# LayerNorm's scale and offset behind the spatial mixing, x added by accumulating loads, and a last product in column halves

## The chip, the cores and the metric

The kernel runs on one core of one Trainium2 chip. The metric is the time of one execution in device microseconds (us), and the kernel's time is the median of several runs. Beside it there is a profile of one execution, in which the engines are called PE (matrix products), DVE (vector engine), ACT (scalar engine with activation functions), POOL (GpSimd) and SP (the engine that issues most DMAs). All of them run their own queue of instructions in order, and wait for each other by semaphores.

## The reference

One layer of a decoder trunk works on 1024 prompt rows and 8 sample rows of width 1024, all in float32. Cut to what matters here:

```
xn = rmsnorm(x, pre_g)
u, v, z_a, x_b, z_b, g_a, g_b = split(xn @ w_in)          # 7 x 1024 columns
vn = layernorm(gelu(v), ln_g, ln_b)                       # scale and offset per channel
s  = tril(w_s[h]) @ vn + b_s[h]                           # within chunks of 128 tokens, 8 channel groups h
y_a = gelu(u) * s * silu(z_a)
y_b = (blockdiag(pool(x_b)) * pool_scale) * silu(z_b)
m  = sigmoid(g_a) * (y_a @ w_pa) + sigmoid(g_b) * (y_b @ w_pb)
h  = x + rmsnorm(m @ w_out, post_g)
y  = h + rmsnorm(sigmoid(rmsnorm(h, ple_in_g) @ w_pg) * (p @ w_ple), ple_out_g)
```

Outputs are y for prompt and samples, the rows vn of the last prompt chunk and of the samples, and two pooling buffers.

## The kernel before

**Products.** Every float32 operand of a large product is cut into two parts of the reduced type float32r, a head (`split`: copied by ACT) and a remainder (subtracted by DVE), and three products of the parts are summed in PSUM. Large products use Strassen's scheme in its form with seven products (`strassen`, line 573): a pair of 128-row blocks takes seven steps P1 to P7, each a run of 24 matmuls of 258 columns (the form `Features`, channels in the partitions) or 12 matmuls of 512 columns (`Tokens`, tokens in the partitions). The sums that Strassen needs are made by DVE, on the weights before a step (`prepare`, line 478) and on the results behind it (`evacuate`, line 581). The seven products go to four regions of PSUM (`r1` to `r4`), for which there are three buffers; P2 is accumulated into the region of P1, P4 into that of P7, P3 into that of P5, so P3 can begin only when P5's result has been read.

**Stages.** The steps stand in one list: V (all four pairs), then the gate GA, U with ZA, XB with ZB, GB, the products with `w_pa` and `w_pb`, the output product (`outsteps`), and the gate product of the embedding (`gatesteps`). Other work is hung behind a step by `at(step, f)`. Weights are fetched six steps ahead (`FETCH`) and prepared three ahead (`AHEAD`).

**The mixing.** V's results are turned to token rows in `big`. In the GA stage (`flow` numbers its 28 steps and U's and ZA's first 14 from 0) every third step takes one token tile: `ln_stats` (mean and variance), `ln_apply` (line 836, two DVE passes over 1024 columns with the rows `lng` and `lnb`), then `v_split`, and `spatial` (line 885), 16 matmuls into four banks `mix` whose two halves are added by DVE, first with `bsb`, the rows of b_s. There are two banks of PSUM for such work. The samples' LayerNorm and mixing stand at `flow` 28 to 30. In the ZA stage, `done` (line 956) multiplies z by u and by the mixed rows in `big`, and `store` spills `ya`.

**The output stage.** `Out` (line 1272) handles the results of the output product: the first quarter (`direct`) is squared and summed by ACT and multiplied by the gain `post` on DVE, the three others (`summed`) are added to `u`, squared and then multiplied by the gain. `out_finish` (line 1297) loads x into `xres`, takes the reciprocal root from POOL (`rstd`), and makes h = result x rstd + x in one DVE pass. `gate_norm` squares h on ACT, takes another `rstd` and scales it to `hn`; `gate_input` transposes `hn` on PE (`pht`) and copies it to `big`. For each pair these stand behind steps 0, 1 and 6 of the next pass. In the embedding's gate product, `gated` (line 1347) takes the sigmoid, multiplies by e and sums squares by halves of 512 columns; `gate_finish` ends a tile: for tiles 0 to 5 one pass and an accumulating load of h issued by POOL, for the last two tiles passes by halves. In the last pair P2 is the last of the seven products (`LAST`).

**The order.** The program's calls aren't issued directly: `Planner` (line 53) records them with their dependencies, simulates them with a duration for each and sets the order of every engine's queue. An operation that isn't part of the fixed opening (`begin`) may start at most `LEAD` (for loads into a fresh buffer: `LOAD`) us ahead of when it is due; `rank` (line 220) picks, among those that could start at the same time, the one that is due first, where due times count for at most `PATIENCE` us behind their place in the program; `SPARE` keeps buffers back from loads. `space` (line 76) says which ranges of a tensor an operation touches. SBUF holds 46 buffers (`slot`) of 1032 columns that all stages share.

Of the kernel before, what the change touches and what calls it, by code (L numbers as in the profile page):

```python
# [21 lines left out]
QT = HT // 2  # L22
HALF = 512
EPS = 1e-6
POOL_BUF = 15
# [27 lines left out]
class Planner:  # L53
# [7 lines left out]
    TABLES = {AF.Gelu_apprx_tanh: 1, AF.Sigmoid: 2, AF.Silu: 3}  # L61
    LOAD, LEAD, PATIENCE, RATE, SPARE = 20.0, 14.0, 30.0, 0.36, 3

# [12 lines left out]
    def space(self, ap):  # L76

        dims, start = list(ap.ap), ap.offset
        if "DRAM" in str(ap.space):
            return ap.tensor.name, 0, 1, ((start, start + sum(s * (n - 1) for s, n in dims) + 1),)  # L80
# [108 lines left out]
    def order(self):  # L189
# [35 lines left out]
        while done < len(self.ops):  # L225
            best = None
            for e in self.ENGINES:
                these = ready[e]
                if fixed[e]:
                    these = [o for o in these if o is fixed[e][-1]]  # L230
                could = [(t, o) for t, o in ((soonest(o), o) for o in these) if t is not None]
                if could:
                    now = min(t for t, _ in could)
                    if best is None or now < best[0]:
                        best = now, min((o for t, o in could if t <= now + 1e-9), key=lambda o: (rank(o), o.seq))
            if best is None:
# [45 lines left out]
def hybrid_step(  # L282
# [222 lines left out]
    class Tokens:  # L505
# [4 lines left out]
        sums = (P, 2, HALF)  # L510

    class Turned(Weights):

# [59 lines left out]
    def strassen(weights, operand, user, form=Features, order=None):  # L573
# [31 lines left out]
        for p, a, b, r in sorted(plan, key=lambda x: order.index(x[0])) if order else plan:  # L605
            def run(p=p, a=a, b=b, r=r):
                new = r not in at
                if new:
                    at[r] = form.new()
                product(form, at[r], weights.ready[a], lambda k: operand.at(b, k), new, True, not new)  # L610

            steps.append(Step(lambda a=a: weights.prepare(a), run, lambda p=p: evacuate(p)))
        steps[0].loads = lambda: (weights.fetch(), user.loads())
# [221 lines left out]

    def ln_apply(t, n=P):
        v = vtok(t)
        nm, r = lnv.pop(t)
        nc.vector.scalar_tensor_tensor(out=v[:n], in0=v[:n], scalar=nm[:n], in1=lnt["g"][:n],
                                       op0=ALU.add, op1=ALU.mult)  # L840
        nc.vector.scalar_tensor_tensor(out=v[:n], in0=v[:n], scalar=r[:n], in1=lnt["b"][:n],
                                       op0=ALU.mult, op1=ALU.add)
        if t == NB - 1:
            dma(o_chunk_v[0, 0], v)
        if t == S:
            dma(o_schunk_v[0, :, 0], v[:n])

    lnt = {}

    def early_loads():  # L850
# [13 lines left out]
    def spatial_weights():  # L864

        ws = lnt["ws"]
        nc.gpsimd.affine_select(out=ws, in_=ws, pattern=[[0, NB], [-1, P]], compare_op=ALU.is_ge,
                                fill=0.0, base=0, channel_multiplier=1)
        lnt["wst"] = []
        for h4 in range(0, NB, 4):  # L870
            w = slot("wst", (P, 4, 2, P), F32R)
            ps = bank("psw")
            for i in range(4):
                nc.tensor.transpose(ps[:, i * P : (i + 1) * P], ws[:, h4 + i, :], ident)
            split(ps.rearrange("p (h t) -> p h t", t=P), w[:, :, 0], w[:, :, 1])
            lnt["wst"].append(w)

    def v_split(t):
# [6 lines left out]
    def spatial(t):  # L885

        vh, vl = lnv.pop(("cut", t))
        for h2 in range(0, NB, 2):
            ps = bank("mix").rearrange("p (h c t) -> p h c t", h=2, c=2)
            for i in range(2):  # L890
# [4 lines left out]
                nc.tensor.matmul(ps[:, i, 0], vl[:, c], w[:, 0], start=False, stop=True)  # L895
            c = slice(h2 * P, (h2 + 2) * P)
            o = big[:, t, c].rearrange("p (h t) -> p h t", h=2)
            add(o, ps[:, :, 0], lnt["bs"][:, c].rearrange("p (h t) -> p h t", h=2))
            add(o, ps[:, :, 1], o)
# [53 lines left out]
    class ZA(User):  # L953
        func = AF.Silu

        def done(self):
            u = us.pop(self.pair)
            for m, z in enumerate(self.out):
                b = 2 * self.pair + m
                mul(z, z, u[m])  # L960
                zt = z[:, :SEQ].rearrange("p (t c) -> p t c", c=P)
                mul(zt, zt, big[:, :, b * P : (b + 1) * P])
                mul(z[:, SEQ:], z[:, SEQ:], smix_s[:, b, :])
# [308 lines left out]
    class Out(User):  # L1272
# [9 lines left out]
        def direct(self, m, j, ps):  # L1282
            t = self.tile(m)
            parts[t].append(square_sum(ps))
            mul(h_of[t][:, half(j)], ps, gains["post"][:, half(j)])

        def summed(self, m, j, ps, u, free):
# [3 lines left out]
            parts[t].append(square_sum(o))  # L1291
            mul(o, o, gains["post"][:, half(j)])

# [40 lines left out]
    def out_sample():  # L1334
        start(S, "hs")
        for j, o in enumerate(sample_product(samples["m"], woop)):
            parts[S].append(square_sum(o[:NS], NS))
            mul(h_of[S][:NS, half(j)], o[:NS], gains["post"][:NS, half(j)])

# [6 lines left out]

    def gated(t, j, src):
        r = rows(t)
        g = ge[t][:r, half(j)]
        nc.scalar.activation(out=g, in_=src, func=AF.Sigmoid)  # L1350
        mul(g, e_of[t][:r, half(j)], g)
        parts[t].append(square_sum(g, r))
        if t >= NB - 2:
            mul(g, g, gains["out"][:r, half(j)])

# [18 lines left out]
    class Embed(User):  # L1374
# [3 lines left out]

        def direct(self, m, j, ps):
            gated(2 * self.pair + m, j, ps)  # L1380

        def summed(self, m, j, ps, u, free):
            t = 2 * self.pair + m
            o = ge[t][:, half(j)]
            add(o, ps, u)
            gated(t, j, o)
            if len(parts[t]) == 2:
# [7 lines left out]
    def embed_gate_sample():  # L1395
        ge_start(S)
        for j, o in enumerate(sample_product(samples["h"], wgop)):
            gated(S, j, o[:NS])
        gate_finish(S)
# [212 lines left out]
```

## Time and profile before

| | us |
|---|---|
| median of three runs | 1040.45 (1040.35 to 1040.99) |
| the profiled execution, whole | 1037.16 |
| its span, from the first to the last instruction | 1035.1 |
| PE busy, DVE busy, ACT busy, POOL busy in the span | 1007.9, 818.8, 475.3, 82.8 |
| mean clock granted to PE, as a share of full speed | 0.992 |
| mean busy share of the 16 DMA engines by the main queue | 45.4% |

The span is what the profile shows of one execution; its own time holds 2.06 us more, outside the first and the last instruction. In the rows of the profile an instruction is written as line, engine, operation, then "output<-inputs" by the names of the tiles; all recorded operations have line 275, that of `play`, so the tile's name tells them apart. A group's row ends with the busy time, the mean in ns, and the idle time of the engine just before, with what ended it. A window's row has its length, the busy time and the number of instructions of each engine, the mean clock of PE, the share of DMA and GB/s. A row in order of time has start, duration, engine, and the number of merged instructions.

### The profile page before, as it was taken

To read this page: it belongs to the slowest core of one execution; us is meant where nothing else is said; L and a number is where in the kernel's file an instruction comes from. 1 tells how busy PE (TensorE), PEld (TensorE's weight loads), DVE (VectorE), ACT (ScalarE), POOL (GpSimd) and SP (SyncE) were. 2 spreads that over 40 slices of the span, in tenths; PEclk is the share of its full clock that TensorE was granted. 3 is DMA by queue.
4 is the path that set the end of the run, shared out by engine and by line. 5 is a ranking of instruction groups with operands and counts; after the bars stand their busy time and mean duration, and the time that the engine had idled before them with its cause. 6 is when DMAs were issued, how large, how long until landed. Compare 5 with 4: busy or idle time off the path is not lost. (4 is left out here: it accounts for less than half of the span.)

```text
span 1035.1 us, 18740 instructions
## 1 busy us (share of the span) xinstructions
PE 1007.9 (97%) x7539; PEld 965.0 (93%) x7539; DVE 818.8 (79%) x1274; ACT 475.3 (46%) x844; POOL 82.8 (8%) x118
## 2 busy tenths in 40 slices
PE   8999997999999999999999999999999999998996
PEld 6999997999999999999999999999999997886885
DVE  5986557999577777776777787697699899989696
ACT  7664354444333434242323343462352364687563
POOL 2200001101000000000010100000000003312122
PEclk9999998999999999999999999999999999999998
DMA  9332564223144625612132167775695562385436
GB/s 341 123 108 86 180 205 143 83 82 109 58 155 171 225 103 164 231 46 92 62 99 100 58 229 250 282 257 204 196 338 205 193 236 83 124 296 212 123 84 203
DMA packets 85059, 169.23 MB, mean 163 GB/s; under 512 B 6370, under 2 KB 46338, under 8 KB 84965
## 3 DMA queue, kind: packets, MB, share of 16 engines
q1 hardware_dynamic: 83789, 164.36, 45.4%
q0 software_dynamic: 864, 3.15, 1.7%
q8 instruction: 59, 0.97, 0.4%
q10 hardware_dynamic: 320, 0.54, 0.2%
q14 instruction: 27, 0.22, 0.1%
HBM read 116.71 MB, written 51.77 MB: 163 GB/s over the span
## 5 line engine op out<-in xcount | busy, mean ns | idle before, releaser
L275 DVE TENSOR_TENSOR u<-acc,u 128x516 f32<-128x516 f32 x106 | 73.4, 692 | 52.1 <-PE acc L275 51.5
L275 POOL TENSOR_TENSOR rstd<-ms,mhalf 128x1 f32<-128x1 f32 (+2 forms) x45 | 56.2, 1253 | 328.2 <-DVE ms L275 325.5
L275 ACT ACTIVATE u<-acc 128x516 f32<-128x516 f32 x39 | 23.4, 600 | 70.6 <-PE acc L275 65.6
L275 ACT ACTIVATE zbw<-zbs 128x512 fp32r<-128x512 f32 x16 | 9.7, 628 | 36.4 <-DVE zbs L275 30.6
L275 POOL COPY big<-xb 128x1 f32<-128x1 f32 x8 | 3.0, 369 | 290.8 <-ACT xb L275 237.4
L275 ACT ACTIVATE paw<-pas 128x512 fp32r<-128x512 f32 x16 | 9.9, 629 | 33.2 <-DVE pas L275 27.0
L275 ACT ACTIVATE pbw<-pbs 128x512 fp32r<-128x512 f32 x16 | 10.0, 631 | 30.1 <-DVE pbs L275 23.4
L275 DVE TENSOR_TENSOR big<-big 128x1032 f32<-128x1032 f32 (+3 forms) x20 | 23.6, 1219 | 0.0
L275 PE MATMUL accm<-qh,wpoolw 128*128 128x258 f32 x128 | 21.8, 285 | 0.4 <-DVE zb L275 0.4
L275 POOL MEMSET mst<- 128x1024 f32 x1 | 1.0, 957 | 257.3 <-PE acct L275 257.3
L275 ACT ACTIVATE gaw<-gas 128x512 fp32r<-128x512 f32 x16 | 10.1, 631 | 23.8 <-DVE gas L275 5.9
L275 ACT ACTIVATE big<-vt 128x256 f32<-128x256 f32 x32 | 11.9, 380 | 18.6 <-PE vt L275 18.6
L275 PE MATMUL mix<-wst,vh 128*128 128x256 f32 x64 | 16.2, 330 | 3.6 <-DVE big L275 2.8
L275 ACT ACTIVATE big<-pht,gvec 128x128 f32<-128x128 f32 x64 | 17.6, 387 | 4.1 <-PE pht L275 4.1
L275 ACT ACTIVATE gbw<-gbs 128x512 fp32r<-128x512 f32 x16 | 9.8, 626 | 20.2 <-DVE gbs L275 16.6
L275 DVE SCALAR_TENSOR_TENSOR zb<-accm,gvec,zb 128x516 f32<-128x516 f32 x16 | 12.0, 751 | 8.7 <-PE accm L275 8.4
L275 ACT ACT_TABLE_LOAD x13 | 16.7, 1283 | 4.8 <-DMA yblow<-yblow 3.8
L275 PEld LDWEIGHTS accm<-qh,wpoolw 128*128 128x128 f32 x128 | 18.1, 190 | 0.8 <-DVE zb L275 0.8
L275 ACT ACTIVATE uw<-us 128x512 fp32r<-128x512 f32 x16 | 9.8, 626 | 19.2 <-DVE us L275 18.2
L275 ACT ACTIVATE zaw<-zas 128x512 fp32r<-128x512 f32 x16 | 9.6, 624 | 17.4 <-DVE zas L275 13.3
L275 ACT ACTIVATE junk<-ge 128x512 bf16<-128x512 f32 (+1 forms) x18 | 11.5, 636 | 12.0 <-DVE ge L275 11.4
L275 PE MATMUL mix<-wst,vl 128*128 128x128 f32 x64 | 14.6, 228 | 2.1 <-DVE vl L275 2.1
(672 smaller groups left out, 3757.5 us busy)
## 6 DMA issues: line engine op xcount, KB each, us to landing
ga<-ga SPq DMA_DIRECT2D x16, 516.0 KB
gb<-gb SPq DMA_DIRECT2D x16, 516.0 KB
ya<-za SPq DMA_DIRECT2D x8, 516.0 KB
yb<-zb SPq DMA_DIRECT2D x8, 516.0 KB
m<-ga SPq DMA_DIRECT2D x8, 516.0 KB
m<-m SPq DMA_DIRECT2D x8, 516.0 KB
x<-in_x_prompt_dram SPq DMA_DIRECT2D x8, 512.0 KB
vraw<-in_w_in_dram SPq DMA_DIRECT2D x8, 512.0 KB
```

Of the source, the lines that this page charges most:

```text
L275: getattr(getattr(self.nc, e), method)(*args, **kwargs)
```

## The change

Five edits go together.

- LayerNorm before the mixing only takes away the mean and divides by the deviation. As the mixing is linear, the channel's scale and offset are applied behind it: mixed x ln_g + (row sum of tril(w_s) x ln_b + b_s). `spatial_offsets` makes the bracket once, with four matmuls of a block of ones with `wst`, and eight DVE operations; `ZA.done` applies both by one DVE pass for each of eight channel blocks. Only the tiles that are outputs (the last tile and the samples) are still scaled before. Between PSUM and `big`, ACT copies the first half of a bank and DVE adds the second. Token tiles come every four steps, and the samples at `flow` 4 to 6.
- In the output stage the results aren't multiplied by the gain; `out_finish` makes result x rstd x gain in its one pass, and x is added to it by an accumulating load that POOL issues.
- The last product (P2 of the last pair) is computed in two halves of 256 columns, each with its own evacuation.
- The planner knows rows and columns of DRAM tensors, may leave an engine idle for a short time when an urgent operation is about to be ready (`SPARED`), and has other constants.
- `gated` takes a range of columns, and adds up two partial sums where there are three.

```diff
@@ Planner
-    LOAD, LEAD, PATIENCE, RATE, SPARE = 20.0, 14.0, 30.0, 0.36, 3
+    LOAD, LEAD, PATIENCE, RATE, SPARE = 17.0, 14.0, 60.0, 0.36, 3
+    SPARED = 1.0
...
+                    o = min((o for t, o in could if t <= now + 1e-9), key=lambda o: (rank(o), o.seq))
+
+                    soon = [(t, u) for t, u in could if now < t < now + o.busy and u.late + slip <= t
+                            and t + u.busy + self.SPARED < o.late + slip]
+                    if soon and not o.fixed:
+                        now, o = min(soon, key=lambda x: (x[0], x[1].seq))
@@ strassen
+            def run_halves(a=a, b=b, r=r):
+                for c in (slice(0, QUART), slice(QUART, HALF)):
+                    product(columns(c), at[r], weights.ready[a], lambda k: operand.at(b, k), False, True, True)
+                    user.direct(0, 0, at[r][:, c], c)
+
+            if order and p == order[-1] == "P2":
+                steps.append(Step(lambda a=a: weights.prepare(a), run_halves, nothing))
@@ ln_apply
-        nc.vector.scalar_tensor_tensor(out=v[:n], in0=v[:n], scalar=nm[:n], in1=lnt["g"][:n],
-                                       op0=ALU.add, op1=ALU.mult)
-        nc.vector.scalar_tensor_tensor(out=v[:n], in0=v[:n], scalar=r[:n], in1=lnt["b"][:n],
-                                       op0=ALU.mult, op1=ALU.add)
...
+        nc.vector.tensor_scalar(out=v[:n], in0=v[:n], scalar1=nm[:n], scalar2=r[:n], op0=ALU.add, op1=ALU.mult)
+        if t in (S, NB - 1):
+            o = sv if t == S else slot("lastv", (P, D))
+            mul(o[:n], v[:n], lnt["g"][:n])
+            add(o[:n], o[:n], lnt["b"][:n])
+            dma(o_schunk_v[0, :, 0] if t == S else o_chunk_v[0, 0], o[:n])
@@ ln_loads
+        for i, v in enumerate((ln_g, ln_b)):
+            dma(vecs[i * NB : (i + 1) * NB, :], v[0].rearrange("(k p) -> k p", p=P))
@@ spatial_weights
+        nc.tensor.transpose(ps[:, : 2 * NB], vecs[: 2 * NB, :], ident[: 2 * NB, : 2 * NB])
+        nc.vector.tensor_copy(lncol, ps[:, : 2 * NB].rearrange("p (i k) -> p i k", i=2))
+
+    def spatial_offsets():
+
+        ones = slot("ones", (P, P), F32R)
+        nc.gpsimd.memset(f32(ones), 1.0)
+        off = lnt["off"] = slot("off", (P, NB, P))
+        for h4, w in zip(range(0, NB, 4), lnt["wst"]):
+            ps = bank("rowsum")
+            for c in range(2):
+                nc.tensor.matmul(ps.rearrange("p (h t) -> p h t", t=P), ones, w[:, :, c], start=c == 0, stop=c == 1)
+            for h in range(h4, h4 + 4):
+                c = slice(h * P, (h + 1) * P)
+                nc.vector.scalar_tensor_tensor(out=off[:, h], in0=ps[:, (h - h4) * P : (h - h4 + 1) * P],
+                                               scalar=lncol[:, 1, h : h + 1], in1=lnt["bs"][:, c],
+                                               op0=ALU.mult, op1=ALU.add)
@@ spatial
-            add(o, ps[:, :, 0], lnt["bs"][:, c].rearrange("p (h t) -> p h t", h=2))
+            nc.scalar.activation(out=o, in_=ps[:, :, 0], func=AF.Copy)
             add(o, ps[:, :, 1], o)
@@ ZA.done
-                mul(zt, zt, big[:, :, b * P : (b + 1) * P])
+                nc.vector.scalar_tensor_tensor(out=mixed, in0=mixed, scalar=lncol[:, 0, b : b + 1],
+                                               in1=lnt["off"][:, b].unsqueeze(1).to_broadcast([P, NB, P]),
+                                               op0=ALU.mult, op1=ALU.add)
+                mul(zt, zt, mixed)
@@ the places in flow
-        s = 3 + 3 * n
+        s = 3 + 4 * n
...
-    at(flow[28], lambda: ln_stats(S, NS))
-    at(flow[29], lambda: ln_apply(S, NS))
-    at(flow[30], sample_spatial)
+    at(flow[4], lambda: ln_stats(S, NS))
+    at(flow[5], lambda: ln_apply(S, NS))
+    at(flow[6], sample_spatial)
+    at(flow[8], spatial_offsets)
@@ Out
-            mul(h_of[t][:, half(j)], ps, gains["post"][:, half(j)])
+            nc.scalar.activation(out=h_of[t][:, half(j)], in_=ps, func=AF.Copy)
...
-            mul(o, o, gains["post"][:, half(j)])
@@ out_finish
-        xs = slot("xres", (P, D))
-        dma(xs[:r], x_of(t))
         rs = rstd(parts.pop(t), r)
-        nc.vector.scalar_tensor_tensor(out=xs[:r], in0=h_of[t][:r], scalar=rs[:r], in1=xs[:r],
-                                       op0=ALU.mult, op1=ALU.add)
-        h_of[t] = xs
-        dma(kept["h"][t * P : t * P + r, :], xs[:r])
+        nc.vector.scalar_tensor_tensor(out=h, in0=h, scalar=rs[:r], in1=gains["post"][:r],
+                                       op0=ALU.mult, op1=ALU.mult)
+        nc.gpsimd.dma_start(out=h, in_=x_of(t), accum_op=ALU.add)
+        dma(kept["h"][t * P : t * P + r, :], h)
@@ gated
+        if len(parts[t]) > 2:
+            a, b = parts[t][:2]
+            both = sm("both")
+            nc.vector.tensor_scalar(out=both[:r], in0=a[:r], scalar1=b[:r], scalar2=None, op0=ALU.add)
+            parts[t][:2] = [both]
```

More of the change, by code (lines that the diff above doesn't have):

```diff
@@ L23 @@
 HALF = 512
+QUART = 256
 EPS = 1e-6
@@ L79, in space @@
         if "DRAM" in str(ap.space):
-            return ap.tensor.name, 0, 1, ((start, start + sum(s * (n - 1) for s, n in dims) + 1),)
+            row = ap.tensor.shape[-1]
+            first, start = divmod(start, row)
+            rows = sum(s // row * (n - 1) for s, n in dims if s >= row)
+            return (ap.tensor.name, first, first + rows + 1,
+                    ((start, start + sum(s * (n - 1) for s, n in dims if s < row) + 1),))
         row, parts = dims[0]
@@ L233, in order @@
                     now = min(t for t, _ in could)
+                    o = min((o for t, o in could if t <= now + 1e-9), key=lambda o: (rank(o), o.seq))
[3 more added lines that the diff above has]
+                        now, o = min(soon, key=lambda x: (x[0], x[1].seq))
                     if best is None or now < best[0]:
-                        best = now, min((o for t, o in could if t <= now + 1e-9), key=lambda o: (rank(o), o.seq))
+                        best = now, o
             if best is None:
@@ L510, in hybrid_step, with columns @@
         sums = (P, 2, HALF)
+    def columns(c):
+        class Part(Tokens):
+            pieces = staticmethod(lambda ps: [(ps[:, c], c)])
+        return Part
     class Turned(Weights):
@@ L610, in run @@
                 product(form, at[r], weights.ready[a], lambda k: operand.at(b, k), new, True, not new)
-            steps.append(Step(lambda a=a: weights.prepare(a), run, lambda p=p: evacuate(p)))
+            def run_halves(a=a, b=b, r=r):
[4 more added lines that the diff above has]
+                steps.append(Step(lambda a=a: weights.prepare(a), run_halves, nothing))
+            else:
+                steps.append(Step(lambda a=a: weights.prepare(a), run, lambda p=p: evacuate(p)))
         steps[0].loads = lambda: (weights.fetch(), user.loads())
@@ L838, in ln_apply @@
         nm, r = lnv.pop(t)
[L839 to L846 removed]
+        nc.vector.tensor_scalar(out=v[:n], in0=v[:n], scalar1=nm[:n], scalar2=r[:n], op0=ALU.add, op1=ALU.mult)
[4 more added lines that the diff above has]
+            dma(o_schunk_v[0, :, 0] if t == S else o_chunk_v[0, 0], o[:n])
     lnt = {}
+    lncol = cpool.tile([P, 2, NB], F32, tag="lncol", name="lncol")
     def early_loads():
@@ L876, in spatial_weights @@
             lnt["wst"].append(w)
+        ps = bank("lncol")
+        nc.tensor.transpose(ps[:, : 2 * NB], vecs[: 2 * NB, :], ident[: 2 * NB, : 2 * NB])
[13 more added lines that the diff above has]
+                                               op0=ALU.mult, op1=ALU.add)
     def v_split(t):
@@ L1337, in out_sample @@
             parts[S].append(square_sum(o[:NS], NS))
-            mul(h_of[S][:NS, half(j)], o[:NS], gains["post"][:NS, half(j)])
+            nc.scalar.activation(out=h_of[S][:NS, half(j)], in_=o[:NS], func=AF.Copy)
     ge, e_of = {}, {}
@@ L1345, in ge_start, with gated @@
         dma(e_of[t][: rows(t)], kept["e"][t * P : t * P + rows(t), :])
-    def gated(t, j, src):
+    def gated(t, c, src):
         r = rows(t)
-        g = ge[t][:r, half(j)]
+        g = ge[t][:r, c]
         nc.scalar.activation(out=g, in_=src, func=AF.Sigmoid)
-        mul(g, e_of[t][:r, half(j)], g)
+        mul(g, e_of[t][:r, c], g)
         parts[t].append(square_sum(g, r))
+        if len(parts[t]) > 2:
[3 more added lines that the diff above has]
+            parts[t][:2] = [both]
         if t >= NB - 2:
-            mul(g, g, gains["out"][:r, half(j)])
+            mul(g, g, gains["out"][:r, c])
     def gate_finish(t):
@@ L1377, in loads, with direct @@
                 ge_start(2 * self.pair + m)
-        def direct(self, m, j, ps):
-            gated(2 * self.pair + m, j, ps)
+        def direct(self, m, j, ps, c=None):
+            gated(2 * self.pair + m, c or half(j), ps)
         def summed(self, m, j, ps, u, free):
@@ L1385, in summed @@
             add(o, ps, u)
-            gated(t, j, o)
+            gated(t, half(j), o)
             if len(parts[t]) == 2:
@@ L1397, in embed_gate_sample @@
         for j, o in enumerate(sample_product(samples["h"], wgop)):
-            gated(S, j, o[:NS])
+            gated(S, half(j), o[:NS])
         gate_finish(S)
```

6 lines of the change are left out of this document (3 added, 3 removed).

## The prediction, made before the changed kernel ran

> **What bounds the kernel now.** I read the page's first block, then a table of windows that I cut at the stages, then PE's waits, then the instructions in order of time at the places found.
>
> ```profile
> span 1035.1 us, 18740 instructions
> ...
> PE 1007.9 (97%) x7539; PEld 965.0 (93%) x7539; DVE 818.8 (79%) x1274; ACT 475.3 (46%) x844; POOL 82.8 (8%) x118
> ```
> ```profile
> core 0: us, PE busy (x) PEld busy (x) DVE busy (x) ACT busy (x) POOL busy (x), PEclk, DMA share, GB/s
> 0.00:25.90 25.90, 20.93 (x117) 17.50 (x118) 14.21 (x32) 19.40 (x31) 7.68 (x30) 1.00 1.01 341
> ...
> 160.50:174.00 13.50, 7.49 (x44) 6.99 (x43) 13.28 (x26) 6.49 (x9) 2.22 (x2) 0.75 0.60 200
> 174.00:206.00 32.00, 32.00 (x270) 32.00 (x269) 28.88 (x59) 14.61 (x23) 3.80 (x3) 1.00 0.23 81
> 206.00:262.00 56.00, 53.85 (x447) 53.40 (x446) 53.02 (x105) 25.76 (x39) 5.96 (x4) 1.00 0.28 96
> 262.00:466.00 204.00, 204.00 (x1695) 204.00 (x1694) 149.18 (x229) 76.33 (x116) 0.97 (x3) 1.00 0.42 144
> 466.00:828.00 362.00, 361.57 (x2997) 361.15 (x2997) 285.97 (x419) 133.83 (x201) 9.87 (x17) 1.00 0.53 183
> ...
> 857.00:945.00 88.00, 87.68 (x408) 71.00 (x407) 81.60 (x130) 62.08 (x140) 21.53 (x16) 1.00 0.53 195
> 945.00:965.00 20.00, 16.01 (x72) 12.81 (x71) 18.56 (x29) 13.09 (x36) 4.12 (x3) 0.91 0.29 106
> ...
> 1026.00:1035.10 9.10, 0.00 (x0) 0.00 (x0) 3.89 (x7) 1.16 (x3) 0.93 (x1) 0.71 0.38 145
> ```
>
> PE is the bound: 27.2 us of the span are left without a matmul. About 5 lie in the first 26 us, whose order is fixed and stays, and 9 behind the last matmul. The rest is what a change of the vector work can touch. The windows say where: in the mixing stage 6.01 us (160.5 to 174) and 2.15 (206 to 262), at the seam between output and gate products 3.99 (945 to 965). In each, DVE is busy 93 to 98% of the time. Where it is busy 73% (262 to 466) or 79% (466 to 828), PE loses 0 and 0.43 us. So PE stands only where DVE is nearly full. PE's waits name the partners:
>
> ```profile
> PE acct L275 <- DVE ms L275: 4.0, 1, 4.0
> PE mix L275 <- DVE big L275: 2.8, 2, 1.4
> PE acc L275 <- ACT u L275: 2.5, 1, 2.5
> PE mix L275 <- DVE vl L275: 2.1, 1, 2.1
> ```
> ```profile
> 158.19 0.69 DVE L275 TENSOR_TENSOR gas<-garaw,garaw 128x512 f32<-128x512 f32 x1 [3.51 <-PE acc L275]
> ...
> 949.96 2.35 DVE L275 TENSOR_TENSOR wgB22l<-wgB,wgB22h 128x1024 fp32r<-128x1024 f32 x2
> 952.23 0.69 DVE L275 TENSOR_TENSOR hw<-hs,hw 128x512 fp32r<-128x512 f32 x1
> 952.83 0.69 DVE L275 TENSOR_TENSOR ge<-acct,u 128x512 f32<-128x512 f32 x1
> ```
>
> At 949 PE needs the weights' remainder `wgB22l`, the remainder `hw` and the PSUM region that `ge<-acct,u` reads; all three end one behind the other on DVE. The stall at 161 has a second root: DVE itself stood 3.5 us until 158.2 for a slot that PE still read, and had a queue afterwards. Fewer DVE instructions don't remove that one by themselves.
>
> PE also ran slower there: at a mean clock of 0.75, 7.49 busy us hold about 7.49 x 0.25 = 1.9 us of slowness, and 16.01 x 0.09 = 1.4 at the seam. Losable in all: 6.0 + 1.9 + 2.15 = 10.1 us in the mixing stage, 4.0 + 1.4 + 0.3 = 5.7 in 857 to 965.
>
> The Trainium skill ("TensorE: Matmul & The Clock Gate", section "HAM oscillation — how this bites in real kernels") says that the clock is kept as long as no idle gap of PE exceeds about 3.4 us. The trace doesn't bear this out here: the longest wait of that window was 2.5 us, and the clock was 0.75. By the page, what remains of the first stall below would cost 1 us less.
>
> **The change part by part.**
>
> ```profile
> L275 DVE SCALAR_TENSOR_TENSOR big<-big,nmean,lng 128x1024 f32<-128x1024 f32 x8 | 10.2, 1279 | 0.0
> L275 DVE SCALAR_TENSOR_TENSOR big<-big,rstd,lnb 128x1024 f32<-128x1024 f32 x8 | 10.2, 1277 | 0.0
> L275 DVE TENSOR_TENSOR big<-mix,bsb 128x256 f32<-128x256 f32 x32 | 12.3, 415 | 0.0
> L275 DVE TENSOR_SCALAR x<-x,rstd 128x1024 f32<-128x1024 f32 x8 | 6.0, 753 | 0.7 <-POOL rstd L275 0.7
> L275 DVE TENSOR_TENSOR za<-za,big 128x1024 f32<-128x1024 f32 x8 | 9.7, 1219 | 0.0
> L275 ACT ACTIVATE big<-vt 128x256 f32<-128x256 f32 x32 | 11.9, 380 | 18.6 <-PE vt L275 18.6
> ```
>
> *LayerNorm and mixing.* Per token tile two passes of 1.28 us become one TENSOR_SCALAR, which has the form of `x<-x,rstd`: 0.75. Four of the eight adds from PSUM go to ACT at about 0.38 each. DVE saves 2.56 - 0.75 + 4 x 0.415 = 3.5 us a tile, 28 in all; ACT gets 12, and was busy 46 to 48% here. Added on DVE: scale and offset of the last tile and the samples (4 passes of 1.22 = 4.9), and eight offset rows of 128 from PSUM (at most the 0.415 of 256 columns, I take 0.28: 2.2). In 174 to 262, DVE's 81.9 of 88 us fall by about 7 x 3.5 = 24, to 66%, and tiles come every 4 steps instead of 3: the 2.15 us go. The start is different. Sample work is moved from steps 28 to 30 to steps 4 to 6, and the offsets stand at step 8, so into the few steps where the first stall is; what is added there (7.1) is about twice what the first tile saves. That, and the slot wait, which stays possible, make me leave half of 6.0 + 1.9: 4.0 stays. **-6.1 us**.
>
> A bank of PSUM is now read by ACT, then DVE. The bounds are 0.4 us less (one add off DVE's queue) and 0.4 more for each of 8 tiles; 2.9 us of other matmuls stand between two pairs of banks, so I take 0.
>
> *Scale and offset behind the mixing* add eight passes with scalar and broadcast row. No row has this form; 1.22 (`za<-za,big`) to 1.28, I take 1.28: 10.2 us in 262 to 466. DVE goes from 149 to 159 of 204 us, 78%, where 79% stood beside PE's 0.43: 0. The pair's chain gets 2.6 us longer; behind it on SP's queue wait the spills of `ya`, for the last pair the state's load into `big`, and weight loads behind those. Their lead covers it; without cover, 4 x 2.6.
>
> *PE.*
>
> ```profile
> 910.01 0.87 PE pht L275 x8
> 910.88 2.79 PE acct L275 x12
> ```
>
> Four matmuls of 128x512 at 2.79/12 and one transpose at 0.87/8 make 1.04. The last product's 24 halves at 204/1695 = 0.12 us are 2.89 for 2.79. **+1.1 us.** Two loads of 4 KB on SP cost nothing on the path.
>
> *Output products.*
>
> ```profile
> L275 DVE TENSOR_TENSOR h<-h,post 128x512 f32<-128x512 f32 x12 | 8.1, 684 | 0.5 <-ACT junk L275 0.5
> L275 DVE TENSOR_TENSOR h<-acct,post 128x512 f32<-128x512 f32 x4 | 2.7, 674 | 0.0
> L275 DVE SCALAR_TENSOR_TENSOR xres<-h,rstd,xres 128x1024 f32<-128x1024 f32 x8 | 10.3, 1284 | 2.5 <-POOL rstd L275 2.4
> L275 ACT ACTIVATE junk<-xres 128x1024 bf16<-128x1024 f32 x8 | 8.4, 1056 | 5.0 <-DVE xres L275 4.9
> L275 POOL TENSOR_TENSOR rstd<-ms,mhalf 128x1 f32<-128x1 f32 x40 | 49.5, 1240 | 289.1 <-DVE ms L275 286.5 <-DVE big L275 2.2
> L275 POOL DMA_DIRECT2D ge<-h x6 | 5.5, 913 | 7.7 <-issue 6.7 <-DVE u L275 1.1
> ```
> ```profile
> DMA to landing us min/median/max: 5.5/7.4/8.5
> ```
>
> Sixteen products with the gain leave DVE (10.8 us, with the samples' two 12.2); the 1.28 us pass stays, with other operands. DVE falls from 100.2 to 88 of 108 us between 857 and 965: 81%, near the stage at 79%. ACT gets six copies of about 0.6, 3.6 us of 108, and holds a region longer by 0.6 in each pair (at most 2.4 on PE; I take 0). So the 5.7 can go. Against it: x was waiting in SBUF and is now added by a load that POOL issues after that pass. The profile has this kind in `ge<-h`: 0.9 to issue, 7.4 to land. The square stood right behind the pass; now 8.3 us lie between. Behind the waiting issue on POOL stand the next tiles' `rstd`, and DVE and ACT wait for those. A pair has from step 0 to step 6 of the next pass, 6 x 2.79 = 16.7 us, before PE meets its transposes. The chain: rstd 1.24, pass 1.28, load 8.3, square 1.06, rstd 1.24, scaling 0.75, 13.9 and a small `ms` before each rstd: just inside, with little left for a second tile. I charge 0.5 us for each of four pairs. **-3.7 us**, bounds -5.7 and +12 (rival 3).
>
> *The end.*
>
> ```profile
> 1025.41 0.40 PE L275 MATMUL acct<-wgB21h,hw 128*128 128x512 f32 x1
> ...
> 1025.85 0.60 ACT L275 ACTIVATE ge<-acct 128x512 f32<-128x512 f32 x1
> ...
> 1026.99 0.68 DVE L275 TENSOR_TENSOR ge<-eback,ge 128x512 f32<-128x512 f32 x1
> 1027.77 0.63 ACT L275 ACTIVATE junk<-ge 128x512 bf16<-128x512 f32 x1 [1.32 <-DVE ge L275]
> ```
>
> With 256 columns these become about 0.38, 0.415 and 0.38: 0.74 less; the other half's steps run beside the last matmuls, and the small sum of two parts beside the square. **-0.7 us**, bounds 0 and -1.1 (the product also queued 0.4 behind another on DVE).
>
> *Planner* (`LOAD` 20 to 17, `PATIENCE`, `SPARED`, finer DRAM ranges): changes the order everywhere, at no price of its own; I take 0. The bound above:
>
> ```profile
> ACT pbw L275 <- DMA pbraw<-in_w_pb_dram: 7.5, 3, 4.5
> ```
>
> ACT already waited three times for weights, hidden by steps prepared ahead; loads 3 us later could show 3 x 3 = 9.
>
> Sum: -6.1 + 1.1 - 3.7 - 0.7 = -9.4. The profiled execution took 1037.16 (2.06 beside its span), so 1027.8; the median shown is 3.29 above that execution, so about 1031.
>
> **The rivals.** (1) *All of it is recovered*: nothing stays of the first stall, the loads land in time: -10.1 + 1.1 - 5.7 - 0.7 = -15.4, 1025. For it: no stall of PE below 90% of DVE. Against: the crowded first steps. (2) *The stalls are of order, not of load*: queues run in the planned order, and a late slot or release stops PE whatever DVE's share is. The new order stalls elsewhere as much, and only 1.1 - 0.7 and some 2 us of the seam remain: 1039 to 1041. For it: DVE's own 3.5 us wait at 158, and 174 to 206 with 90% and no stall. If the first half of the last product were read only when the second is done, the edit wouldn't do what it says: 0.7 more. (3) *The accumulating load comes too late*, the case on the other side: transposes stand in PE's order and wait. It decides against the change from about 3 us per pair (the other terms are -6.1 + 1.1 - 5.7 - 0.7 = -11.4, over four pairs). With landings of 8.5 and the second tile behind the first by another 0.9 + 1.28 + 1.24, a pair is late by some 4 to 4.5, 18 us: 1047. For it: 13.9 of 16.7 us are used up in the mean. Against: `ge<-h` landed in 5.5 at best, and PE may have other passes first.
>
> The Trainium skill ("DMA: Bandwidth & Descriptors", section "SWDGE vs HWDGE vs iDMA") states that GpSimd writes descriptors into SBUF, from which DVE's two-port mode locks it out, and that loads issued by SP are immune. That speaks for rival 3; here the six issues took 0.91 us on average on a busy DVE, so I don't raise its price.
>
> **How the numbers follow.** Forecast 0.50, rival 1 0.18, rival 2 0.15, rival 3 and late weight loads 0.17. Some 0.2% (2 us) is what a measurement can tell from no change, so faster than 1038.4 is 0.70, within 0.12, slower 0.18. The range runs from 1023, past rival 1, to 1044, where part of the third case is left out.
>
> **What would show it.** Right: windows of the mixing stage with DVE at 70% and PE's idle under 5 us, at the seam under 2; last matmul to end shorter by 0.7. Wrong: PE waiting for `hn` or `pht` in the output stage, DVE waiting for a DMA into `h`, `mix` waiting for `vl` as before, or weights late in 466 to 828.

## The result, and the profile after

| | before, us | after, us |
|---|---|---|
| median of four runs each | 1040.49 (1040.35 to 1040.99) | 1029.64 (1028.6 to 1029.87) |
| the profiled execution, whole | 1037.16 | 1029.87 |
| its span | 1035.1 | 1028.1 |

The ratio of after to before is 0.9893, with a 95% interval of 0.9876 to 0.991: the change saves 10.9 us by the medians. The two profiled executions differ by 7.3 only. Of the 82 executions of the kernel before in the jobs of the experiments (1036.66 to 1043.56 us), 27 took less than 1039 us, at a mean granted clock of 0.989 to 0.993, and 55 took more, at 0.986 to 0.991, and the profiled one, at 0.992, is of the first kind; so differences of a stage below, which are those of this pair, leave 3.6 of the 10.9 us without a place. The changed kernel's four executions have 0.992 to 0.994. By an estimate from these rows, a clock lower by 0.005 over 1008 us of matmuls is 5 us; where it may be lost is read from `out_alone` below.

First the page of the changed kernel: span, busy time and share of each engine.

```profile
span 1028.1 us, 18781 instructions
...
PE 1010.2 (98%) x7556; PEld 966.9 (94%) x7556; DVE 801.7 (78%) x1239; ACT 490.1 (48%) x885; POOL 76.8 (7%) x128
```

Then its windows, cut at the same places as before (the columns are those of the table before; the last row begins at the new last matmul's end).

```profile
0.00:25.90 25.90, 21.08 (x114) 17.65 (x115) 13.88 (x32) 19.00 (x30) 7.68 (x30) 0.93 0.98 336
160.50:174.00 13.50, 12.62 (x79) 12.22 (x78) 9.31 (x22) 6.95 (x12) 0.42 (x1) 0.75 0.17 52
174.00:206.00 32.00, 31.95 (x265) 31.68 (x264) 29.74 (x63) 17.99 (x32) 2.47 (x4) 1.00 0.75 259
206.00:262.00 56.00, 56.00 (x470) 56.00 (x470) 43.14 (x82) 32.08 (x57) 2.08 (x3) 1.00 0.27 89
262.00:466.00 204.00, 204.00 (x1696) 203.97 (x1695) 159.49 (x240) 78.25 (x120) 0.95 (x3) 1.00 0.44 153
466.00:828.00 362.00, 358.83 (x2966) 357.48 (x2965) 284.87 (x417) 133.76 (x200) 9.86 (x17) 1.00 0.52 180
857.00:945.00 88.00, 87.73 (x409) 71.26 (x407) 74.04 (x116) 66.66 (x151) 23.48 (x26) 1.00 0.68 200
945.00:965.00 20.00, 19.34 (x91) 15.70 (x92) 18.21 (x31) 15.72 (x41) 5.43 (x5) 1.00 0.26 98
1020.50:1028.10 7.60, 0.01 (x1) 0.00 (x0) 3.84 (x9) 1.29 (x5) 0.60 (x1) 0.60 0.38 139
```

PE is still the bound, with 17.9 us of idle time in place of 27.2. The pair's difference can be told window by window, as PE's idle time plus the slowness (busy time times one less the clock):

| where | before | after | difference | forecast |
|---|---|---|---|---|
| mixing, 160.5 to 262 | 6.0 + 1.9 + 2.15 = 10.1 | 0.88 + 12.62 x 0.25 + 0.05 = 4.1 | -6.0 | -6.1 |
| output and seam, 857 to 965 | 5.7 | 0.27 + 0.66 = 0.9 | -4.8 | -3.7 |
| end: behind the last matmul 9.3 and 7.6, and a new wait of 0.5 between its halves | 9.3 | 8.1 | -1.2 | -0.7 |
| 466 to 828 | 0.4 | 3.2 | +2.7 | 0 |
| PE's added work (2.2 us more busy, less 1.3 of slowness) | | | +0.9 | +1.1 |
| opening, 0 to 25.9 | 5.0 | 4.8 + 21.08 x 0.07 = 6.3 | +1.3 | 0 |

The sum is -7.1, and the spans differ by 7.0. But for rounding the two must agree, since a span is PE's busy and idle time: the table places the difference, it doesn't test it. The opening has a fixed order that the change leaves alone; its loss is a clock of 0.93 in this execution where the other had 1.00.

PE's waits after, its own rows in us in total, times, and the longest:

```profile
PE accm L287 <- DVE zb L287: 1.7, 2, 1.4
...
PE acct L287 <- ACT ge L287: 1.0, 2, 0.5
PE mix L287 <- DVE big L287: 0.9, 1, 0.9
PE acc L287 <- ACT pbw L287: 0.9, 1, 0.9
...
PE acct L287 <- DVE ms L287: 0.5, 1, 0.5
PE accm L287 <- DVE ql L287: 0.4, 1, 0.4
```

The four waits quoted before the change are gone or small: `mix` for `vl` and `acc` for `u` no longer appear, `big` falls from 2.8 to 0.9, and the seam's `ms` from 4.0 to 0.5. New are `zb`, `ql` and `pbw`, all in 466 to 828. The one for `pbw` (0.9 us, at 794.6) goes back to a late weight load: ACT, which makes `pbw`, had stood 2.46 us until 792.03 for the load of `pbraw`, and DVE 0.72 us for the same. No wait for `hn` or `pht` is among them. ACT's squares of h waited for the accumulating loads three times, 1.8 us in all; no wait of PE names them. This is their row in the view of the DMAs, with the median from issue to landing, beside the kind from which I had taken its price:

```profile
h<-in_x_prompt_dram POOLq DMA_DIRECT2D x8, 512.0 KB, 6.1
...
ge<-h POOLq DMA_DIRECT2D x6, 512.0 KB, 5.7
```

The end in order of time (start, duration, engine):

```profile
1018.76 0.38 ACT L287 ACTIVATE ge<-acct 128x256 f32<-128x256 f32 x1 [0.41 <-PE acct L287]
...
1019.19 0.39 PE L287 MATMUL acct<-wgB21h,hw 128*128 128x256 f32 x1 [0.47 <-ACT ge L287]
...
1020.24 0.28 PE L287 MATMUL acct<-wgB21h,hw 128*128 128x256 f32 x1
...
1020.55 0.38 ACT L287 ACTIVATE ge<-acct 128x256 f32<-128x256 f32 x1 [0.72 <-PE acct L287]
```

ACT reads the first half at 1018.76, while the second still has to be computed: the edit does what it says. But PE stands 0.47 us until that read has ended, though it writes other columns.

### The profile page after: what moved, and what is told of

It reads as the page before. It is cut to its first block, busy times and chain, and to the rows that moved or that the text cites. A ratio compares the mean times of both kernels' runs of the same rounds, so it can differ in the third digit from the quotient of the medians.

```text
span 1028.1 us, 18781 instructions
## 1 busy us (share of the span) xinstructions
PE 1010.2 (98%) x7556; PEld 966.9 (94%) x7556; DVE 801.7 (78%) x1239; ACT 490.1 (48%) x885; POOL 76.8 (7%) x128
## 5 line engine op out<-in xcount | busy, mean ns | idle before, releaser
L287 POOL TENSOR_TENSOR rstd<-ms,mhalf 128x1 f32<-128x1 f32 (+2 forms) x45 | 41.6, 927 | 231.3 <-DVE ms L287 208.4
L287 ACT ACTIVATE big<-mix 128x256 f32<-128x256 f32 x32 | 12.1, 382 | 22.1 <-PE mix L287 18.5
L287 ACT ACTIVATE junk<-h 128x512 bf16<-128x512 f32 (+1 forms) x20 | 16.3, 815 | 11.6 <-DVE h L287 9.7
L287 DVE TENSOR_TENSOR big<-mix,big 128x256 f32<-128x256 f32 x32 | 13.1, 421 | 10.1 <-ACT big L287 9.8
L287 ACT ACTIVATE big<-pht,gvec 128x128 f32<-128x128 f32 x64 | 17.9, 396 | 4.2 <-PE pht L287 4.2
```

The lines of the kernel that those rows point to most:

```text
L287: getattr(getattr(self.nc, e), method)(*args, **kwargs)
```

## The experiments

Each run stands beside runs of the kernel before on the same chip. Those had medians between 1039.34 and 1040.31 in the four jobs, so about 1 us between medians of different jobs isn't told apart.

| run | median us | ratio to before, 95% interval |
|---|---|---|
| the changed kernel | 1029.64 | 0.9893 (0.9876 to 0.991) |
| mix_alone: before with the mixing edit | 1032.73 | 0.9922 (0.9901 to 0.9943) |
| out_alone: before with the output edit | 1037.91 | 0.9978 (0.9964 to 0.9993) |
| plan_alone: before with the planner edit | 1041.27 | 1.0012 (0.9998 to 1.0025) |
| no_mix: after without the mixing edit | 1036.33 | 0.997 (0.9957 to 0.9983) |
| no_out: after without the output edit | 1035.16 | 0.9957 (0.9942 to 0.9972) |
| no_plan: after without the planner edit | 1033.45 | 0.9933 (0.991 to 0.9956) |
| no_halves: after without the halves | 1030.8 | 0.991 (0.9891 to 0.9928) |
| two_banks: halves in two banks | 1030.37 | 0.9912 (0.9891 to 0.9933) |
| two_tiles: halves in two buffers | 1029.19 | 0.9902 (0.9884 to 0.992) |
| x_by_dve: x added by DVE | 1036.3 | 0.9972 (0.9961 to 0.9983) |
| samples_late: samples back at steps 28 to 30 | 1038.17 | 0.9988 (0.9974 to 1.0001) |
| hold_rows: four buffers kept | 1040.04 | 1.0003 (0.9991 to 1.0014) |

### The mixing edit alone, and without it

`mix_alone` has, of the change, the first edit whole (`ln_apply`, `ln_loads`, `spatial_weights`, `spatial_offsets`, `spatial`, `ZA.done`, the places in `flow`) and nothing else.

```diff
-        s = 3 + 3 * n
+        s = 3 + 4 * n
...
-    at(flow[28], lambda: ln_stats(S, NS))
+    at(flow[4], lambda: ln_stats(S, NS))
...
+    at(flow[8], spatial_offsets)
```

> The kernel before with only the LayerNorm and mixing edit (and the places in flow that go with it); output stage, last product and planner as before. If the stalls come from the vector engine's load, the edit brings its own part wherever it stands: the forecast's terms -6.1 + 1.1 = -5.0 us, so about 1035.5 us, with less than 5 us of PE idle between 155 and 265 us of the span and the stall at the seam (about 950) as before. If the stalls come from the order of the queues, the edit alone does little or moves the stall: 1038 to 1043.

`no_mix` takes the same lines out of the changed kernel.

> The changed kernel with the LayerNorm and mixing edit undone. By load: 5 us slower than the changed kernel, about 1034.6, with PE idle again in 155 to 265 us. By order (the planner's settings remove the stalls): about 1031.

Alone the edit saved 7.4 us; taken out of the change, 6.7 were missing. Both are on the side of the load theory, and both are more than its 5.0. The mixing stage as one window, before:

```profile
155.00:270.00 115.00, 106.85 (x870) 105.89 (x869) 101.42 (x197) 50.63 (x76) 11.98 (x8) 0.97 0.29 98
```

`mix_alone`, with the seam below it:

```profile
155.00:270.00 115.00, 113.39 (x916) 112.82 (x915) 89.75 (x175) 62.65 (x112) 5.39 (x8) 0.97 0.31 102
...
935.00:965.00 30.00, 26.06 (x109) 20.94 (x108) 25.16 (x40) 21.69 (x55) 6.48 (x5) 0.89 0.31 116
```

and `no_mix`:

```profile
155.00:270.00 115.00, 107.56 (x857) 105.78 (x856) 103.95 (x199) 49.70 (x73) 10.58 (x8) 0.97 0.35 121
```

PE's idle time of this stage, 8.2 us before, is 1.6 with the edit alone and 7.4 without it. The seam keeps its 3.9 us in `mix_alone`: the two stalls are independent, and the one in the mixing stage goes with the mixing edit. Which of its parts does it (the passes saved on DVE, ACT's share, a tile every four steps) was not taken apart.

A part of what the medians show and the profiled pair doesn't may lie here too. `out_alone` has the mixing stage of before, and its profiled execution is one with a low clock (1039.22 us, 0.989):

```profile
155.00:270.00 115.00, 107.28 (x849) 106.33 (x849) 100.79 (x196) 49.78 (x74) 11.97 (x8) 0.94 0.29 100
```

PE's idle time is much the same as before, but the clock is 0.94 where it was 0.97: 107.28 x 0.06 = 6.4 us of slowness for 106.85 x 0.03 = 3.2, some 3 us more. One trace is not enough to show that this is the missing 3.6.

### The output edit alone, and without it

```diff
-            mul(h_of[t][:, half(j)], ps, gains["post"][:, half(j)])
+            nc.scalar.activation(out=h_of[t][:, half(j)], in_=ps, func=AF.Copy)
...
+        nc.vector.scalar_tensor_tensor(out=h, in0=h, scalar=rs[:r], in1=gains["post"][:r],
+                                       op0=ALU.mult, op1=ALU.mult)
+        nc.gpsimd.dma_start(out=h, in_=x_of(t), accum_op=ALU.add)
```

> The kernel before with only the output edit (gain in out_finish, x by an accumulating load). By load: -3.7 us, about 1036.8, with the 4 us stall at the seam gone and the mixing stage as before. By order: 1040 or slower, with the stall moved. If the accumulating load is late, PE waits for hn in the output stage and the time is over 1041.

> The changed kernel with the output edit undone (gains applied at once, x loaded ahead). By load: 3.7 us slower, about 1033.3, with a stall of PE of some 4 us at the seam. By order: within 1 us of the changed kernel.

Alone it saved 2.2 us, less than the 3.7 of the load theory, and the change without it lacks 5.5, more than that. Without it the seam stands as before; `no_out`'s first wait of PE:

```profile
PE acct L287 <- DVE ms L287: 3.9, 1, 3.9
```

With it alone, the wait for `ms` goes, but PE meets others in the same stage (`out_alone`'s waits):

```profile
PE acct L275 <- DVE u L275: 1.8, 1, 1.8
PE acct L275 <- ACT junk L275: 1.4, 2, 1.0
...
PE acct L275 <- DVE hw L275: 0.9, 1, 0.9
```

They sum to 4.1, about as much as was removed. None is for the transposes. The largest goes back to an accumulating load all the same: ACT's square `junk` of h stood 4.13 us for it, DVE's `ms` behind that, and PE behind `u`, the next evacuation on DVE's queue.

```profile
926.39 1.06 ACT L275 ACTIVATE junk<-h 128x1024 bf16<-128x1024 f32 x1 [4.13 <-DMA h<-in_x_prompt_dram]
...
927.58 0.15 DVE L275 TENSOR_SCALAR ms<-ssq 128x1 f32<-128x1 f32 x1 [3.14 <-ACT junk L275]
...
930.89 0.50 PE L275 MATMUL acct<-woT4h,mw 128*128 128x512 f32 x1 [1.76 <-DVE u L275]
```

In all, ACT's squares stand 7.7 us for these loads here, in five waits, and 1.8 in the changed kernel.

### The planner edit alone, and without it

```diff
-    LOAD, LEAD, PATIENCE, RATE, SPARE = 20.0, 14.0, 30.0, 0.36, 3
+    LOAD, LEAD, PATIENCE, RATE, SPARE = 17.0, 14.0, 60.0, 0.36, 3
+    SPARED = 1.0
```

(with the ranges of DRAM tensors and the rule of `SPARED`, as in the change.)

> The kernel before with only the planner's edits (LOAD, PATIENCE, SPARED, rows and columns of DRAM tensors). By load: 1040 within 2 us, since no engine gets less to do. By order: most of the gain is here, 1031 to 1035.

> The changed kernel with the planner's edits undone. By load: within 1 us of 1029.6. By order: 1035 or more, with new stalls in the mixing stage or at the seam.

Alone it made no difference that these runs can tell (1.0012, with 1 in the interval). Its trace moves stalls about; these are `plan_alone`'s waits:

```profile
PE mix L286 <- DVE vl L286: 4.0, 4, 1.3
PE acct L286 <- DVE ms L286: 3.9, 1, 3.9
...
PE accm L286 <- DVE zb L286: 1.7, 2, 1.4
```

The wait for `zb` that the changed kernel shows in 466 to 828 is here already, and PE loses 3.6 us in that window (358.42 busy of 362), against 0.6 in `no_plan` (361.42). So the new loss of 2.7 us comes with the planner's new order, not with the mixing or the output. Yet the change without the planner edit is 3.8 us slower by the medians, where the two theories had at most 1 or at least 5. The intervals just touch, and two of its six executions, 1029.63 and 1030.8, are close to the changed kernel's; the trace is that of the slowest, 1034.44. Its waits:

```profile
PE acct L276 <- DVE u L276: 2.2, 1, 2.2
...
PE acct L276 <- ACT junk L276: 1.0, 1, 1.0
```

These are `out_alone`'s waits again, and the one for `u` has the same origin: ACT's squares stand 7.3 us for the accumulating loads here, the longest time 4.7. Between the two traces, the new order takes 3.6 us of PE's idle time out of 857 to 965 and 2.4 in smaller pieces ahead of it (160.5 to 262, 262 to 466, 828 to 857), and adds 2.6 in 466 to 828. The two edits are worth more together than their single runs add up to.

### The last product's halves

`no_halves` has the last product in one piece of 512 columns, and `gated` without its range of columns.

```diff
-            if order and p == order[-1] == "P2":
-                steps.append(Step(lambda a=a: weights.prepare(a), run_halves, nothing))
-            else:
-                steps.append(Step(lambda a=a: weights.prepare(a), run, lambda p=p: evacuate(p)))
+            steps.append(Step(lambda a=a: weights.prepare(a), run, lambda p=p: evacuate(p)))
```

> The changed kernel with the last product undivided, as before. The forecast gave the halves 0.7 us less behind the last matmul and 0.1 more on PE: 1030.2 against the changed kernel's 1029.6. The changed kernel's trace shows PE standing 0.47 us between the halves, for ACT's read of the first; by that the halves bring only 0.2 and this run ends at 1029.8.

By the medians that costs 1.2 us, which the intervals don't separate, and so neither of the two forecasts; the trace does tell it. From the last matmul to the end lie 8.7 us, and 7.6 with the halves. Two runs then asked what the 0.47 us between the halves hang on. `two_banks` puts them into the two PSUM banks of one `region`, `two_tiles` into two buffers.

```diff
-            pieces = staticmethod(lambda ps: [(ps[:, c], c)])
+            pieces = staticmethod(lambda ps: [(ps[:, q, :QUART], c)])
```

> The changed kernel with the two halves of the last product in two banks of PSUM (P1 and P2 of the last pair write columns 0 to 255 to one bank, 256 to 511 to the other). If PE's wait of 0.47 us between the halves is the price of sharing a bank, it goes, and the last matmul ends about 0.7 us earlier: 1029.0. If the wait goes by the whole buffer and not by the bank, nothing changes but 12 more matmuls of half the width for P1: 1029.7.

```diff
+                if new and order and order[-1] == "P2" and r == "r1":
+                    at[r] = region("acct")[:, 0], bank("acctb")
```

> The changed kernel with the two halves of the last product in two buffers of PSUM (P1 and P2 of the last pair; the second half takes one of the small banks). The halves in two banks of one buffer left PE's wait of 0.47 us as it was. If the wait goes by the buffer, it is gone here, the last matmul ends about 0.7 us earlier and the time is 1029.0. If PE waits for something else (ACT's read as such), it stays and the time is 1029.6 or a little more.

With two banks the wait is unchanged (`two_banks`, the second half's first matmul):

```profile
1019.69 0.39 PE L287 MATMUL acct<-wgB21h,hw 128*128 128x256 f32 x1 [0.47 <-ACT ge L287]
```

With two buffers it is gone: of two waits of `acct` for `ge` one is left, 0.5 us, elsewhere. So in this program the wait goes by the buffer and not by the bank. At 1029.19 this version has the lowest median, but its interval covers the changed kernel's.

### x added on DVE

Rival 3 fell with the first trace, as far as the changed kernel goes. What the accumulating load is worth, with the gain kept in `out_finish`, was asked by one more DVE pass for each tile:

```diff
+        xs = slot("xres", (P, D))
+        dma(xs[:r], x_of(t))
...
-        nc.gpsimd.dma_start(out=h, in_=x_of(t), accum_op=ALU.add)
+        add(h, h, xs[:r])
```

> The changed kernel with x loaded ahead by SP and added by one more DVE pass per tile (1.22 us) in place of the accumulating load. If the gain of the output edit comes from DVE's load, DVE goes from 92 to 102 us of 108 between 857 and 965, and most of the stall at the seam is back: 1032 to 1034. If the landing time of the accumulating load had eaten part of the gain, this one is as fast or faster: 1027 to 1029.

It was slower than either theory had it: 6.7 us behind the changed kernel, more than `no_out`, which has no such load either. Its waits have the seam back:

```profile
PE acct L287 <- DVE ms L287: 4.5, 1, 4.5
```

The load on the path that I feared is what carries the edit: without it nothing of the edit's gain is left. Whether by the DVE pass or by the buffer `xres` that it saves, this run can't say; DVE is busy for 96.6 of 108 us between 857 and 965, between the changed kernel's 92.3 and the 102 that were expected.

### Samples at the old place

The forecast took the samples' work at steps 4 to 6 for a burden on the crowded start. This run puts it back.

```diff
-    at(flow[4], lambda: ln_stats(S, NS))
-    at(flow[5], lambda: ln_apply(S, NS))
-    at(flow[6], sample_spatial)
+    at(flow[28], lambda: ln_stats(S, NS))
+    at(flow[29], lambda: ln_apply(S, NS))
+    at(flow[30], sample_spatial)
```

> The changed kernel with the samples' LayerNorm and mixing back at flow 28 to 30 (their offsets of the last tile stay). In the changed kernel PE runs at half clock from about 165.6 to 171.9 us, right behind the samples' eight tiny products and a wait of 0.88 us. If the samples' work at the start causes wait and half clock, both go and some 3 to 4 us with them: 1026. If any short break does it (the first tile's mixing always has one), the half clock stays and the time too: 1029 to 1030.

Both theories were wrong: 8.5 us slower than the changed kernel. The half clock at 166 to 172 did go, as the first had it, but other stalls came. The mixing stage of `samples_late`:

```profile
155.00:270.00 115.00, 106.72 (x849) 105.19 (x849) 85.73 (x169) 59.21 (x103) 5.97 (x8) 0.97 0.37 126
```

PE loses 8.3 us, as much as before the change, beside a DVE that is busy 75% of the time (88% before). One part can be followed in order of time:

```profile
180.00 0.38 SPq L287 DMA_DIRECT2D lnb<-in_ln_b_dram  x1
181.31 0.41 SPq L287 DMA_DIRECT2D garaw<-in_w_in_dram  x1
...
187.09 0.43 SPq L287 DMA_DIRECT2D garaw<-in_w_in_dram  x1
188.94 0.63 ACT L287 ACTIVATE gaw<-garaw 128x512 fp32r<-128x512 f32 x1 [0.78 <-DMA garaw<-in_w_in_dram]
...
189.62 0.73 PE L287 MATMUL acc<-xB11h,gaw 128*128 128x258 f32 x2 [1.43 <-ACT gaw L287]
```

ACT waits for the weights `garaw`, and PE for what ACT makes of them. The changed kernel issues these two loads together:

```profile
174.38 2.01 SPq L287 DMA_DIRECT2D garaw<-in_w_in_dram  x2
```

That is 7 and 13 us earlier. A load into a new tile needs a free one of the 46 buffers. With the samples late, the rows `lng`, `lnb` and `bsb` and the samples' v stay needed for 22 to 24 steps more; here `lnb` itself is not loaded before 180.00. That the loads were late for want of a buffer is argued here, not seen.

### Four buffers kept

That suggested a direct test: leave the changed kernel as it is, but let four buffers of 46 stay taken until step 30, by copies that read one column of each (work that isn't part of the computation).

```diff
+    held = cpool.tile([P, 4], F32, tag="held", name="held")
+    at(flow[30], lambda: [nc.vector.tensor_copy(held[:n, i : i + 1], v[:n, :1]) for i, (v, n) in
+                          enumerate(((lnt["g"], P), (lnt["b"], P), (lnt["bs"], P), (sv, NS)))])
```

> The changed kernel, samples early, with four tiny copies added behind step 30 of flow, which read one column each of the rows lng, lnb and bsb and of the samples' sv: so these four buffers of the 46 stay taken until there, as with the late samples, and DVE gets some 0.6 us more. If the late samples' 8.5 us come from buffers held, so that weight loads are issued late (182 instead of 174 us for the third gate pair), the same stalls come back here: 1034 to 1038, with DVE or ACT waiting for garaw. If they come from the place of the samples' own work, this one stays at 1029.6 to 1030.6.

The whole gain is gone: 1040.04, a ratio of 1.0003. That is on the side of the buffers, and beyond the 1034 to 1038 expected there. The mixing stage of `hold_rows` (its profiled execution took 1042.32, 2.3 above the median):

```profile
155.00:270.00 115.00, 105.64 (x834) 104.17 (x833) 86.43 (x172) 58.13 (x103) 8.53 (x8) 0.94 0.34 116
```

PE loses 9.4 us with DVE at 75%. The waits of the same window, in the order of that view:

```profile
PE mix L287 <- DVE smixs L287: 4.2, 1, 4.2
...
PE acc L287 <- ACT gaw L287: 2.4, 1, 2.4
```

The loads of `garaw` that stood at 174.38 start here at 190.04 and 191.46, but no engine is seen waiting for them, so late weight loads, which I had expected, are not what stops PE. Both waits go back to buffers all the same, at least in part. For the first, DVE's queue shows it (PE's wait ends at 169.18); for the second, ACT's (PE's wait ends at 229.95):

```profile
168.30 0.69 DVE L287 TENSOR_TENSOR gas<-garaw,garaw 128x512 f32<-128x512 f32 x1 [3.31 <-DMA ga<-ga]
168.91 0.22 DVE L287 TENSOR_TENSOR smixs<-smix,bsb 128x64 f32<-128x64 f32 x1
...
229.26 0.63 ACT L287 ACTIVATE gaw<-gas 128x512 fp32r<-128x512 f32 x1 [1.31 <-DMA ga<-ga]
```

`gas` and `gaw` are new tiles here and take no data from `ga`. What they wait for can only be a buffer out of which `ga` is still being stored to DRAM; `smixs`, which PE needs, only stands behind `gas` on DVE's queue. In the changed kernel the same two stand there in the same order, at 161.93 and 163.87, and `gas` waits 0.30 us, for PE. The four copies themselves run at 255 us, behind both stalls.

So the mixing gain needs the buffers that the change frees early. Of the 9.4 us, the stalls of 4.2 and 2.4 are followed to waits of DVE and ACT for a buffer, 3.31 and 1.31 us; the rest is not, and as the planner makes a new order whenever a buffer's life changes, a part of it may be order. Buffers freed in the kernel before, without the saving on DVE, were not tried.

## Why the prediction came out right, point by point

- **The number.** 1031.0 was forecast, 1029.64 measured. That it came so close is partly luck. For the profiled execution 1027.8 was forecast and 1029.87 measured, 2.1 more, as the pair differs by 7.3 and not by my 9.4. Then I added 3.29 for the median, as if the changed kernel's median lay as far above its profiled execution as before; it lies 0.23 below. The two errors have opposite signs.
- **The mixing, -6.1.** -6.0 in the profile, and 6.7 to 7.4 by the runs with and without the edit (these hold most of PE's added 1.1 as well, so the forecast there was -5.0). I had left 4.0, half of the first stall and half of its slowness; 4.0 stayed in 160.5 to 174, but as 0.9 of stall and 3.2 of clock.
- **The step that failed** stands at the head of the prediction: "PE stands only where DVE is nearly full." 174 to 206 has DVE at 93% and PE idle for 0.05 us, and before the change it had 90% and no stall, which I named for rival 2 only; `samples_late` and `hold_rows` have DVE at 75% in the mixing stage, and PE loses 8.3 and 9.4. The saving on DVE isn't shown to be enough. Buffers that come free early are necessary: my 3.5 us "for a slot that PE still read" were the sign of it, and I counted that as the part that would stay. I charged the samples' early place as a cost, and it carries the gain.
- **DVE at 66% in 174 to 262.** It was 72.88 of 88 us, 83%. The saving of the tiles came about as reckoned, but I forgot that the planner fills the place: eight sums of `woraw`, 5.5 us, which stood elsewhere before, and 3.3 us for the offsets and the last tile's row, which I had put at the start.
- **Scale and offset in 262 to 466.** Forecast 159 us of DVE and no idle PE; measured 159.49 and none, each pass at 1280 ns.
- **The output products, -3.7.** -4.8 in the profile; 2.2 alone and 5.5 when taken out. The 0.5 a pair for the accumulating load wasn't due: landing took 6.1 in the median where I put 7.4, and no wait of PE names it. DVE stayed at 92.3 of 108 us, 85%, where I put 81%. The stalls that the edit brings under the old order (`u`, `junk`, `hw`) I hadn't priced; the planner edit removes them.
- **The planner, 0.** Right for the edit alone, while in the change it is worth 3.8 us by the medians, at the edge of the noise: it takes 3.6 from the output stage and 2.4 ahead of it, and gives 2.6 back in 466 to 828. My bound there was for late weights; 0.9 of it is that (`pbw`), the rest is `zb` and `ql`.
- **The end, -0.7.** -1.7 behind the last matmul, less 0.5 for the wait between the halves, which I hadn't seen. The doubt whether the first half would be read early was unfounded.
- **The rivals.** Rival 3 is refuted for the changed kernel: no wait for `hn` or `pht`. Its mechanism exists under the old order: one late load costs PE 1.8 us in `out_alone` and 2.2 in `no_plan`, by way of ACT's and DVE's queues and not of the transposes. That is far from the 18 it was priced at. Rival 1 was too good: neither the first stall nor 466 to 828 is free of loss. Rival 2 was wrong in its time and right in a good part of its reason: in the mixing stage PE stands for buffers that are not yet free, at 75% of DVE too.

## What to carry to other kernels

Ahead of pricing a saved instruction, list which buffers a change frees, and when: where one pool feeds every stage, whether buffers come free in time can decide whether the saved instructions count at all, and a stall beside a busy engine may be a missing buffer in disguise. Where a planner makes the order, run each edit both alone and taken out of the whole, since here two edits were worth 2.2 us and nothing alone, and 5.5 and 3.8 in company.

## What the runs showed of the hardware that was not expected

The granted clock fell to half for some 6 us though PE had stood for less than a microsecond. The changed kernel has one such stretch, here a window of 2 us (PE's clock is the first of the last three columns):

```profile
166.00:168.00 2.00, 2.00 (x10) 2.00 (x11) 1.97 (x7) 0.00 (x0) 0.00 (x0) 0.50 0.03 8
```

The clock is 0.82 in the 2 us before this window, and 0.50 until 172. The pause at its start is 0.88 us, up to 165.71. In `two_tiles` the fall comes with no pause at all in front of it: the clock drops between 162 and 164 and is 0.50 from 164 to 170, while PE's only wait there, 0.16 us, ends at 165.32.

```profile
162.00:164.00 2.00, 2.00 (x17) 1.98 (x17) 1.66 (x4) 0.59 (x2) 0.00 (x0) 0.87 0.00 0
```

What both have in front of the fall are sixteen products of 8x8 for the samples, here of `two_tiles`:

```profile
161.43 1.95 PE L287 MATMUL smix<-diag,sv 8*128 8x8 f32 x16
```

In `samples_late`, which has none there, a wait of 1.20 us at nearly the same time left the clock at 1.00 from 160 to 188:

```profile
162.70 0.33 PE L287 MATMUL mix<-wst,vl 128*128 128x128 f32 x1 [1.20 <-DVE vl L287]
```

That speaks for the small products having a part in it. They are not the only way to it: the kernel before has none there, and its clock fell to 0.50 at 166, behind 6 us in which PE was busy for 2.5. No run tried the small products by themselves, so it stays open. The Trainium skill ("TensorE: Matmul & The Clock Gate", section "HAM oscillation — how this bites in real kernels") puts the limit of an idle gap at about 3.4 us; in these traces shorter ones were no protection.

Loads of 512 KB that add to SBUF, issued by POOL, took 877 to 1053 ns to issue and 6.1 us to land, in a stage in which DVE was busy 85% of the time (92.25 of 108 us).
